# Memory key steps between the row tiles of the output projection, later transposes behind it, more weight chunks in work, and every low part on VectorE

## The chip, the cores and the metric

The kernel runs on one core of one Trainium2 chip. The metric is device time in microseconds of one execution, the median of several runs; less is better. Engines are named as in the profile: PE is TensorE's matmul (PEld its weight load), DVE is VectorE, ACT is ScalarE, POOL is GpSimd and SP is SyncE, which issues the loads.

## The reference

Two layers of a decoder trunk, batch 1, 512 tokens, width 1024, all in float32. Each of a layer's three parts ends in a LayerNorm of `alpha * x + f(x)`:

```python
for l in range(DEPTH):                       # 2
    h = hybrid_mixer(x, ...)                 # u = x @ w_in; branches A, B, C; merged @ w_out
    x = layer_norm(alpha * x + h, ...)
    x = layer_norm(alpha * x + memory_cross_attention(x, mem, xq, xkv, xo), ...)
    x = layer_norm(alpha * x + swiglu(x, w_up, w_down), ...)
```

Branch A is differential attention, C a dilated window attention, and B a recurrence whose two gates come of block-diagonal 64 x 64 products of a convolved input. The three are projected, gated and summed; `w_out` (1024 x 1024) follows. Cross-attention has 4 heads over 256 memory tokens: `k, v = split(mem @ xkv)`, and q comes from the new x. The feed-forward part is 2816 wide.

## The kernel before

**Precision.** PE works on pairs. Every operand is split into a high part in the fast float format (`xh`, `whi`) and a low part, the float32 value less the high part (`xl`, `wlo`). A product is three matmuls: high x high, high x low and low x high.

**Weights.** All weights lie in memory as 371 chunks of 128 x 1024, in the order of their use. For each chunk SP loads `raw` (`load_raw`, L264), ACT casts it to `whi` (`split_chunk`, L272), and `flush` (L282) makes `wlo` by a subtraction at L284: on DVE, but on POOL for the chunks in `on_pool` (L258), which are the memory key chunks 2 to 7 and the first four of `w_up`, ten per layer. `refill` (L289) casts the next chunks after a step, at most two, as long as fewer than `pairs` of the step are in work; `flush` follows after the step's matmuls are written. Loads run three chunks ahead of the casts.

**Steps.** `make_program` (L57) writes out the order of all steps by hand. Kind "a" is one output tile of 128 columns with the weights stationary (`tile_step`, 24 matmuls, 512 wide, or 256 for the memory); kind "b" is one row tile of 128 tokens and 512 columns (`group`, one step for each of the four row tiles, 24 matmuls); "k" does two slices of the contraction for all four rows. A step's result is used by its `post` function, which is written when the next step is. Every engine works through its own list in the order in which it is written, so an instruction waits for all that stands before it on its engine.

**The output projection.** The steps of a layer go: branches; two memory key steps; `w_out` for columns 0 to 511 (four rows) and for 512 to 1023 (four rows); the other six memory key steps; memory values (four rows); queries `xq`. `post_memk` casts a key tile on ACT (`mkh`) and subtracts on DVE (`mkl`). `post_ln` (L688) adds a row to x on DVE (L695) and takes its statistics; at the second half of a row it starts `ln_item` (L487): aggregate, a power on POOL (L492), and two passes over 1024 columns on DVE (L495, L497). `ln_item` then waits some turns (`waits`, L698: three for the first LayerNorm, one or two for the others) before it issues eight transposes of the row on PE (L510), and four casts (ACT) and four subtractions (DVE, L517) make the new `xh` and `xl`. The queries need all four rows. The second LayerNorm (behind `xo`) goes the same way; the first up steps after it take rows 0 and 1 first.

**Branch B.** For each of eight tiles of 128 channels `b_item` (L522) casts the convolved input into `xs`, copies halves across by DMA, and subtracts the two halves of `pad` (64 x 512 each): one on POOL (L534), one on DVE (L535). Four matmuls follow (`z`, L539 and L540). POOL also does `ti` (L565), `bl` (L575), `acc` (L646) and two rotary products per tile (L585, L586).

Of the kernel before, what the change touches and what calls it, by code (L numbers as in the profile page):

```python
# [17 lines left out]
P = 128  # L18
# [38 lines left out]
def make_program():  # L57
# [10 lines left out]
    def tile_step(name, l, c0, act, post, n0=0, n1=S, **kw):  # L68
        c = ch(name, l, 0, KT, c0, P)
        st = Step("a", [c], act=act, post=post, nk=KT, ncol=P, off=0, n0=n0, n1=n1, **kw)  # L70
        steps.append(st)
        return st

    def group(name, l, k0, nk, c0, act, post, pairs, tokens=NT, needs=None, pre=None):
        cs = [ch(name, l, k0 + 2 * k, 2, c0, 512) for k in range(nk // 2)]
        for t in range(tokens):
            st = Step("b", cs, act=act, post=post + (t,), t=t, pairs=pairs)
            if needs:
                st.need = tuple(n.format(t=t) for n in needs)
            if pre and t == 0:  # L80
                st.pre = pre
            steps.append(st)

    for l in range(L):
        def a_head(h, pairs):
# [54 lines left out]
        for n in range(KT):  # L140
            tile_step("w_br_b", l, P * n, "oB", ("merge", l, "B", n), need=("oB%d" % l,),
                      pre=("mem", l) if n == 5 else None)
        for kt in range(2):
            tile_step("xkv", l, P * kt, "mem", ("memk", l, kt), n0=0, n1=MEM, pairs=5)
        for h in range(2):
            group("w_out", l, 0, KT, 512 * h, "m", ("ln", l, 1, h), 5,
                  needs=("m%d" % l,))
        for kt in range(2, KT):
            tile_step("xkv", l, P * kt, "mem", ("memk", l, kt), n0=0, n1=MEM, pairs=5)
        for h in range(2):  # L150
            group("xkv", l, 0, KT, D + 512 * h, "mem", ("memv", l, h), 5, tokens=2)
        for kt in range(KT):
# [2 lines left out]
        for h in range(4):  # L155
            steps.append(Step("k", [ch("xo", l, 2 * h, 2, 0, 512)], act="ox", k0=2 * h,
                              post=("lns", l, 2, 0) if h == 3 else None, pairs=4,
                              need=("ox%d_%d" % (l, h),)))
        group("xo", l, 0, KT, 512, "ox", ("ln", l, 2, 1), 6)
        for gi, (j0, nj) in enumerate(GROUPS):  # L160
            if gi == 0:
                cs = [ch("w_up", l, 0, KT, HID * (i % 2) + P * (i // 2), P) for i in range(4)]
# [17 lines left out]
def kernel(  # L180
# [72 lines left out]
    for s, st in enumerate(steps):  # L253
        for c in st.chunks:
            last_use[c] = s
            if first_use[c] is None:
                first_use[c] = s
    on_pool = {c for c, (name, l, k0, nk, c0, n) in enumerate(chunks)  # L258
               if (name == "xkv" and 2 * P <= c0 < D) or (name == "w_up" and c0 % HID < 2 * P)}
    raws, hi, lo, late = {}, {}, {}, []  # L260
    ptr = {"raw": 0, "split": 0}
    RAW_AHEAD = 3
# [9 lines left out]
    def split_chunk(s):  # L272
        c = ptr["split"]
        while ptr["raw"] <= c:
            load_raw()
        h, lw, raw = a4("whi", [1024], F32R), a4("wlo", [1024], F32R), raws.pop(c)
        A.copy(h, raw)  # L277
        hi[c], lo[c] = h, lw
        late.append((lw, raw, h, G if c in on_pool else V))
        ptr["split"] += 1  # L280

    def flush():  # L282
        for lw, raw, h, eng in late:
            eng.tensor_tensor(lw, raw, f(h), ALU.subtract)  # L284
        late.clear()
        while ptr["raw"] < min(NCH, ptr["split"] + RAW_AHEAD):
            load_raw()
# [199 lines left out]
    def ln_item(l, which, t, waits):  # L487
        st, xt = lnst.pop(t), x_res[t]
        gb, bb = lnp["g"], lnp["b"]
        V.bn_aggr(st[:, 12:14], st[:, 0:12])  # L490
        V.tensor_scalar(st[:, 14:15], st[:, 13:14], EPS_LN, None, ALU.add)  # L491
        G.tensor_tensor(st[:, 15:16], st[:, 14:15], expo, ALU.pow)  # L492
        last = l == L - 1 and which == 3
        for c in (slice(0, 512), slice(512, 1024)) if last else (slice(0, 1024),):
            V.scalar_tensor_tensor(xt[:, c], xt[:, c], st[:, 12:13], gb[:, c],  # L495
                                   ALU.subtract, ALU.mult)
            V.scalar_tensor_tensor(xt[:, c], xt[:, c], st[:, 15:16], bb[:, c],  # L497
                                   ALU.mult, ALU.add)
            if last:
                nc.sync.dma_start(out[t * P:(t + 1) * P, c], xt[:, c])  # L500
        if last:
            return
        for _ in range(waits):
            yield
        if t == 0:
            new_act("x", KT)
        for q in range(2):
            tp = bank("tp")
            for k in range(4):
                T.transpose(tp[:, k * P:(k + 1) * P],  # L510
                            xt[:, (4 * q + k) * P:(4 * q + k + 1) * P], ident)
            for k in range(2):
                xh, xl = acts["x"][2 * q + k]
                src = tp[:, 2 * k * P:2 * (k + 1) * P].rearrange("p (a b) -> p a b", a=2)
                dh, dl = xh[:, :, t * P:(t + 1) * P], xl[:, :, t * P:(t + 1) * P]
                A.copy(dh, src)  # L516
                V.tensor_tensor(dl, src, f(dh), ALU.subtract)  # L517
        mark("x%d_%d_%d" % (l, which, t))
# [3 lines left out]
    def b_item(l, n):  # L522
# [8 lines left out]
        nc.sync.dma_start(f(xs[w, 0, :]), f(xs[u, 0, :]))  # L531
        nc.sync.dma_start(f(xs[u, 1, :]), f(xs[w, 1, :]))
        xl = padded()
        G.tensor_tensor(xl[u, 0, :], xc[u], f(xs[u, 0, :]), ALU.subtract)  # L534
        V.tensor_tensor(xl[w, 1, :], xc[w], f(xs[w, 1, :]), ALU.subtract)  # L535
        yield
        z = [bank("z0"), bank("z1")]
# [150 lines left out]
    def post_ln(ps, l, which, half, t):  # L688
# [6 lines left out]
        V.scalar_tensor_tensor(xs, ps, co, xs, ALU.mult, ALU.add)  # L695
        V.bn_stats(lnst[t][:, 6 * half:6 * half + 6], xs)
        if half == 1:
            waits = 3 if which == 1 else 2 if t == NT - 1 else 1  # L698
            g = ln_item(l, which, t, waits)
            if step_side(g):  # L700
                fresh.append(g)
# [358 lines left out]
```

## Time and profile before

| | |
|---|---|
| median of 3 runs | 2204.24 us (2202.59 to 2205.01) |
| the profiled execution | 2206.34 us, span 2204.6 us |
| PE busy | 2176.7 us |
| DVE busy | 1229.3 us |
| ACT busy | 927.2 us |
| POOL busy | 314.9 us |
| low parts (L284) on DVE | 351, mean 1273 ns |

Times in rows are microseconds from the first instruction of the profiled execution. Busy time of PE overlaps itself: matmuls are pipelined and their ends are modelled, so the distance of two starts tells more than one duration. Idle time is put down to the instruction that released the wait last. `PEclk` is the clock that TensorE was granted, as a share of full speed.

### The profile page before, as it was taken

Reading aid. Unit: us, or ns where it says so; the run is one execution under the profiler, and the core shown is the slowest. Engines: PE = TensorE matmul, PEld = TensorE weight load, DVE = VectorE, ACT = ScalarE, POOL = GpSimd, SP = SyncE. Lnnn points to the kernel's source line nnn. Section 1 sums busy time; section 2 is a strip of 40 time slices with the busy share of each in tenths; the row PEclk is TensorE's granted clock in tenths of the full one; section 3 lists DMA queues with packets and bytes.
Section 4 is the critical chain, followed back from the end, with each engine's and each line's share of the span. In section 5 each row is a group of like instructions: output and inputs, shape, how many; then the busy total and the mean of one; then the engine's idle time right before and its main releaser. Section 6 shows DMA issues by size and latency. Waiting matters only on the chain.

```text
span 2204.6 us, 26795 instructions
## 1 busy us (share of the span) xinstructions
PE 2176.7 (99%) x10516; PEld 1812.0 (82%) x10516; DVE 1229.3 (56%) x2014; ACT 927.2 (42%) x1647; POOL 314.9 (14%) x224
## 2 busy tenths in 40 slices
PE   9999999999999999999999999999999999999998
PEld 6888888788887888888888888887888878888887
DVE  6566666746746733243557676576466466332435
ACT  4445686643334222132135556766333333221330
POOL 3113213310300300000012132032103002000000
PEclk9999999999999999999999999999999999999999
DMA  7213333334332322242242223223334223223321
GB/s 257 79 58 100 96 91 96 117 96 146 107 113 96 108 84 86 69 148 88 72 144 77 66 85 101 85 86 129 105 125 143 86 86 125 78 76 132 97 96 39
DMA packets 65278, 224.37 MB, mean 102 GB/s; under 512 B 7936, under 2 KB 7936, under 8 KB 65152
## 3 DMA queue, kind: packets, MB, share of 16 engines
q1 hardware_dynamic: 65152, 222.66, 31.0%
q8 instruction: 83, 1.36, 0.2%
q14 instruction: 43, 0.35, 0.0%
HBM read 212.14 MB, written 2.10 MB: 97 GB/s over the span
## 4 chain that ended last, share of the span: by engine, by line
PE 70%; issue 22%; POOL 4%; DVE 3%; ACT 1%; DMA 0%; POOLq 0%; SPq 0%; ACTq 0%
PE ps L832 17%; PE ps L831 17%; PE ps L833 16%; PE ps L864 5%; PE ps L862 5%; PE ps L863 5%; POOL wlo L284 2%; PE o L429 1%; PE tp L423 1%; PE sc L356 1%; PE sc L355 1%; POOL ln L492 1%; PE o L385 1%; DVE x L497 1%; POOL bl L575 1%
## 5 line engine op out<-in xcount | busy, mean ns | idle before, releaser
L831 PE MATMUL ps<-xh,whi 128*128 128x512 f32 (+1 forms) x1792 | 695.8, 388 | 2.2 <-ACT xh L891 2.1
L832 PE MATMUL ps<-xl,whi 128*128 128x512 f32 (+1 forms) x1792 | 689.1, 385 | 0.6 <-DVE xl L769 0.5
L833 PE MATMUL ps<-xh,wlo 128*128 128x512 f32 (+1 forms) x1792 | 688.0, 384 | 1.3 <-POOL wlo L284 1.3
L284 DVE TENSOR_TENSOR wlo<-raw,whi 128x1024 fp32r<-128x1024 f32 x351 | 441.7, 1273 | 49.8 <-ACT whi L277 42.3
L277 ACT CAST whi<-raw 128x1024 fp32r<-128x1024 f32 x371 | 382.1, 1045 | 149.2 <-PE ps L863 96.9
L833 PEld LDWEIGHTS ps<-xh,wlo 128*128 128x128 f32 x1792 | 338.9, 189 | 68.6 <-POOL wlo L284 2.1
L831 PEld LDWEIGHTS ps<-xh,whi 128*128 128x128 f32 x1792 | 339.0, 189 | 68.1 <-ACT xh L891 4.4
L832 PEld LDWEIGHTS ps<-xl,whi 128*128 128x128 f32 x1792 | 339.1, 189 | 64.4 <-DVE xl L769 1.0
L492 POOL TENSOR_TENSOR ln<-ln,expo 128x1 f32<-128x1 f32 x24 | 33.8, 1410 | 1182.1 <-DVE ln L491 1182.1
L862 PE MATMUL ps<-whi,hh 128*128 128x512 f32 x352 | 137.3, 390 | 0.0
L863 PE MATMUL ps<-wlo,hh 128*128 128x512 f32 x352 | 137.1, 390 | 0.0
L864 PE MATMUL ps<-whi,hl 128*128 128x512 f32 x352 | 137.1, 390 | 0.0
L759 ACT CAST hh<-fg 128x512 fp32r<-128x512 f32 x44 | 27.3, 620 | 191.8 <-DVE fg L758 191.8
L516 ACT CAST xh<-tp 128x256 fp32r<-128x256 f32 x80 | 28.0, 376 | 178.4 <-PE tp L510 101.3
L748 DVE SCALAR_TENSOR_TENSOR fg<-fg,ps 128x512 f32<-128x512 f32 x44 | 30.3, 688 | 116.9 <-ACT fg L747 116.9
L758 DVE TENSOR_TENSOR fg<-fg,ps 128x512 f32<-128x512 f32 x44 | 30.3, 688 | 114.4 <-PE ps L833 114.4
L747 ACT ACTIVATE fg<-ps 128x512 f32<-128x512 f32 x44 | 26.3, 598 | 135.0 <-PE ps L833 135.0
L585 POOL TENSOR_TENSOR raw<-raw,tabs 128x512 f32<-128x512 f32 x32 | 42.7, 1335 | 254.1 <-ACT raw L582 254.1
L695 DVE SCALAR_TENSOR_TENSOR x<-ps,x 128x512 f32<-128x512 f32 x48 | 33.0, 687 | 80.5 <-PE ps L864 80.4
L863 PEld LDWEIGHTS ps<-wlo,hh 128*128 128x128 f32 x352 | 66.1, 188 | 13.7
L862 PEld LDWEIGHTS ps<-whi,hh 128*128 128x128 f32 x352 | 66.1, 188 | 13.6
L864 PEld LDWEIGHTS ps<-whi,hl 128*128 128x128 f32 x352 | 66.1, 188 | 13.6
(235 smaller groups left out, 3511.7 us busy)
## 6 DMA issues: line engine op xcount, KB each, us to landing
raw<-in_wts_dram SPq DMA_DIRECT2D x371, 512.0 KB, 3.6
xs<-xs SPq DMA_DIRECT2D x32, 128.0 KB, 2.2
lng<-in_lnp_in_dram SPq DMA_DIRECT2D x6, 512.0 KB, 5.0
lnb<-in_lnp_in_dram SPq DMA_DIRECT2D x6, 512.0 KB, 5.7
tabs<-in_tabs_in_dram SPq DMA_DIRECT2D x4, 512.0 KB, 8.9
x<-in_x_in_dram SPq DMA_DIRECT2D x4, 512.0 KB, 8.7
qkA<-qkA SPq DMA_DIRECT2D x16, 128.0 KB, 2.2
qkC<-qkC SPq DMA_DIRECT2D x16, 128.0 KB, 2.2
```

The lines of the kernel that those rows point to most:

```text
L277: A.copy(h, raw)
L284: eng.tensor_tensor(lw, raw, f(h), ALU.subtract)
L492: G.tensor_tensor(st[:, 15:16], st[:, 14:15], expo, ALU.pow)
L585: G.tensor_tensor(raw, raw, tab[:, 0, :], ALU.mult)
L695: V.scalar_tensor_tensor(xs, ps, co, xs, ALU.mult, ALU.add)
L748: V.scalar_tensor_tensor(g, g, 1.0, ps, ALU.add, ALU.mult)
L831: T.matmul(pv, wh, xh, start=(kt == 0), stop=False)
L832: T.matmul(pv, wh, xl, start=False, stop=False)
L833: T.matmul(pv, wl, xh, start=False, stop=(kt == st.nk - 1))
L862: T.matmul(ps, xh, wh, start=(i == 0), stop=False)
L863: T.matmul(ps, xh, wl, start=False, stop=False)
L864: T.matmul(ps, xl, wh, start=False, stop=(i == n - 1))
```

## The change

Four things change. (1) Of the six late memory key steps five now stand between the rows of the second half of `w_out`: one behind row 0, two behind row 1, one behind row 2, two behind row 3. (2) The first LayerNorm's transposes wait until the last row of `w_out` has been taken up (mark `rows`), and row t then for t turns more. (3) `pairs`, the number of chunks in work, goes from 5 to 6 in these steps and from 6 to 8 in the second half of `xo`. (4) `on_pool` is gone: all low parts of weights are made on DVE, as is the other half of `pad`: per layer ten subtractions of 128 x 1024 and eight of 64 x 512 move from POOL to DVE. The list of loads on SP keeps its order.

```diff
+    def group(..., pre=None, between=None):
...
             steps.append(st)
+            if between:
+                between[t]()
...
-        for kt in range(2):
-            tile_step("xkv", l, P * kt, "mem", ("memk", l, kt), n0=0, n1=MEM, pairs=5)
-        for h in range(2):
-            group("w_out", l, 0, KT, 512 * h, "m", ("ln", l, 1, h), 5,
-                  needs=("m%d" % l,))
-        for kt in range(2, KT):
-            tile_step("xkv", l, P * kt, "mem", ("memk", l, kt), n0=0, n1=MEM, pairs=5)
+        def memk(*kts):
+            for kt in kts:
+                tile_step("xkv", l, P * kt, "mem", ("memk", l, kt), n0=0, n1=MEM, pairs=6)
+
+        memk(0, 1)
+        group("w_out", l, 0, KT, 0, "m", ("ln", l, 1, 0), 6, needs=("m%d" % l,))
+        group("w_out", l, 0, KT, 512, "m", ("ln", l, 1, 1), 6, needs=("m%d" % l,),
+              between=(lambda: memk(2), lambda: memk(3, 4), lambda: memk(5), lambda: memk(6, 7)))
...
-        group("xo", l, 0, KT, 512, "ox", ("ln", l, 2, 1), 6)
+        group("xo", l, 0, KT, 512, "ox", ("ln", l, 2, 1), 8)
...
-    on_pool = {c for c, (name, l, k0, nk, c0, n) in enumerate(chunks)
-               if (name == "xkv" and 2 * P <= c0 < D) or (name == "w_up" and c0 % HID < 2 * P)}
...
-        late.append((lw, raw, h, G if c in on_pool else V))
+        late.append((lw, raw, h))
...
-        for lw, raw, h, eng in late:
-            eng.tensor_tensor(lw, raw, f(h), ALU.subtract)
+        for lw, raw, h in late:
+            V.tensor_tensor(lw, raw, f(h), ALU.subtract)
...
             return
+        if which == 1:
+            while not met("rows%d" % l):
+                yield
+            waits = t
         for _ in range(waits):
...
-        G.tensor_tensor(xl[u, 0, :], xc[u], f(xs[u, 0, :]), ALU.subtract)
+        V.tensor_tensor(xl[u, 0, :], xc[u], f(xs[u, 0, :]), ALU.subtract)
...
-            waits = 3 if which == 1 else 2 if t == NT - 1 else 1
+            waits = 2 if t == NT - 1 else 1
+            if which == 1 and t == NT - 1:
+                mark("rows%d" % l)
```

The order of the instructions is made by this list of steps, so three places of it are shown, all in layer 0. Tile names carry a running number; `x_66` to `x_69` are rows 0 to 3 of x. Line numbers from L74 on are larger by up to 7 in the changed kernel.

On PE, at the end of row 0 of the second half of `w_out` (`mh`, `ml` are here the merged activations, 512 wide; the memory is 256 wide). Before, row 1 follows:

```order
L862 MATMUL ps_891_4726<-whi_885_4711,mh_847_4468 128x512
L863 MATMUL ps_891_4726<-wlo_886_4712,mh_847_4468 128x512
L864 MATMUL ps_891_4726<-whi_885_4711,ml_848_4469 128x512
L862 MATMUL ps_894_4761<-whi_868_4581,mh_811_4240 128x512
L863 MATMUL ps_894_4761<-wlo_869_4582,mh_811_4240 128x512
L864 MATMUL ps_894_4761<-whi_868_4581,ml_812_4241 128x512
```

Now memory key step 2 follows, which needs the low part `wlo_893`:

```order
L869 MATMUL ps_891_4726<-whi_886_4714,mh_847_4468 128x512
L870 MATMUL ps_891_4726<-wlo_887_4715,mh_847_4468 128x512
L871 MATMUL ps_891_4726<-whi_886_4714,ml_848_4469 128x512
L838 MATMUL ps_898_4770<-mh_834_4390,whi_892_4751 128x256
L839 MATMUL ps_898_4770<-ml_835_4391,whi_892_4751 128x256
L840 MATMUL ps_898_4770<-mh_834_4390,wlo_893_4752 128x256
```

Rows and key steps now alternate; the number of matmuls is the same.

On DVE, behind the last pass over row 3 in the first LayerNorm (`xl` are the splits of a transposed row, `mkl` the key tiles, `wlo` the low parts). Before:

```order
L497 SCALAR_TENSOR_TENSOR x_69<-x_69,ln_4723,lnb_4620 128x1024
L517 TENSOR_TENSOR xl_4867<-tp_4874,xh_4866 128x2x128
L517 TENSOR_TENSOR xl_4869<-tp_4874,xh_4868 128x2x128
L517 TENSOR_TENSOR xl_4871<-tp_4883,xh_4870 128x2x128
L517 TENSOR_TENSOR xl_4873<-tp_4883,xh_4872 128x2x128
L723 TENSOR_TENSOR mkl_4542<-ps_4892,mkh_4541 128x256
L723 TENSOR_TENSOR mkl_4542<-ps_4931,mkh_4541 128x256
L517 TENSOR_TENSOR xl_4867<-tp_4970,xh_4866 128x2x128
L517 TENSOR_TENSOR xl_4869<-tp_4970,xh_4868 128x2x128
L517 TENSOR_TENSOR xl_4871<-tp_4979,xh_4870 128x2x128
L517 TENSOR_TENSOR xl_4873<-tp_4979,xh_4872 128x2x128
L284 TENSOR_TENSOR wlo_4966<-raw_4958,whi_4965 128x1024
```

Now:

```order
L498 SCALAR_TENSOR_TENSOR x_69<-x_69,ln_4723,lnb_4623 128x1024
L522 TENSOR_TENSOR xl_5005<-tp_5012,xh_5004 128x2x128
L522 TENSOR_TENSOR xl_5007<-tp_5012,xh_5006 128x2x128
L522 TENSOR_TENSOR xl_5009<-tp_5021,xh_5008 128x2x128
L522 TENSOR_TENSOR xl_5011<-tp_5021,xh_5010 128x2x128
L285 TENSOR_TENSOR wlo_4992<-raw_4891,whi_4991 128x1024
L285 TENSOR_TENSOR wlo_4995<-raw_4924,whi_4994 128x1024
L730 TENSOR_TENSOR mkl_4544<-ps_5030,mkh_4543 128x256
L285 TENSOR_TENSOR wlo_5062<-raw_4989,whi_5061 128x1024
L285 TENSOR_TENSOR wlo_5065<-raw_5057,whi_5064 128x1024
L730 TENSOR_TENSOR mkl_4544<-ps_5069,mkh_4543 128x256
```

The two pairs of `wlo` are the low parts of the first memory value rows; they now stand between row 3 and the splits of row 1, and the six key tiles' low parts, which POOL made before, stand further up on DVE.

On DVE in the second LayerNorm, behind the last pass over row 1 (L497, now L498). Before, the splits of row 0 are followed by row 2:

```order
L497 SCALAR_TENSOR_TENSOR x_67<-x_67,ln_6111,lnb_6107 128x1024
L517 TENSOR_TENSOR xl_6197<-tp_6204,xh_6196 128x2x128
L517 TENSOR_TENSOR xl_6199<-tp_6204,xh_6198 128x2x128
L517 TENSOR_TENSOR xl_6201<-tp_6213,xh_6200 128x2x128
L517 TENSOR_TENSOR xl_6203<-tp_6213,xh_6202 128x2x128
L695 SCALAR_TENSOR_TENSOR x_68<-ps_6222,x_68 128x512
```

Now a pair of low parts of `w_up` stands between:

```order
L498 SCALAR_TENSOR_TENSOR x_67<-x_67,ln_6111,lnb_6107 128x1024
L522 TENSOR_TENSOR xl_6203<-tp_6210,xh_6202 128x2x128
L522 TENSOR_TENSOR xl_6205<-tp_6210,xh_6204 128x2x128
L522 TENSOR_TENSOR xl_6207<-tp_6219,xh_6206 128x2x128
L522 TENSOR_TENSOR xl_6209<-tp_6219,xh_6208 128x2x128
L285 TENSOR_TENSOR wlo_6190<-raw_6102,whi_6189 128x1024
L285 TENSOR_TENSOR wlo_6193<-raw_6185,whi_6192 128x1024
L700 SCALAR_TENSOR_TENSOR x_68<-ps_6228,x_68 128x512
```

Another pair stands in the same way behind row 0's last pass, ahead of row 1. Before, these four were made on POOL. The order of the transposes among the rows and up steps on PE is the same as before in this place.

## Rows read from the trace of the kernel before

**Rows 1.** The page, part 1: busy us (share of the span) and instructions
```profile
PE 2176.7 (99%) x10516; PEld 1812.0 (82%) x10516; DVE 1229.3 (56%) x2014; ACT 927.2 (42%) x1647; POOL 314.9 (14%) x224
```

**Rows 2.** Waits of PE: engine, line <- waited for: us in total, times, longest
```profile
PE ps L833 <- POOL wlo L284: 5.0, 6, 1.9
...
PE z L540 <- POOL pad L534: 4.4, 2, 2.2
...
PE tp L510 <- DVE x L497: 3.1, 2, 1.5
```

**Rows 3.** Timeline of PE, last B gates of layer 0: start, us, what [idle before <-releaser]
```profile
437.56 0.39 PE L833 MATMUL ps<-xh,wlo 128*128 128x512 f32 x1
...
437.79 0.39 PE L539 MATMUL z<-xs,gw 128*128 128x512 f32 x1
...
440.40 0.50 PE L540 MATMUL z<-pad,gw 128*128 128x512 f32 x1 [2.22 <-POOL pad L534]
```

**Rows 4.** Timeline of PE in a memory key step of layer 0
```profile
577.48 0.28 PE L831 MATMUL ps<-mh,whi 128*128 128x256 f32 x1
...
577.60 0.28 PE L832 MATMUL ps<-ml,whi 128*128 128x256 f32 x1
...
579.75 0.39 PE L833 MATMUL ps<-mh,wlo 128*128 128x256 f32 x1 [1.88 <-POOL wlo L284]
```

**Rows 5.** Sums by window: us, then PE, PEld, DVE, ACT, POOL busy, PEclk, DMA share, GB/s
```profile
441.10:444.50 3.40, 3.40 (x10) 2.65 (x9) 1.02 (x2) 3.31 (x5) 0.00 (x0) 0.50 0.59 176
...
581.10:584.50 3.40, 3.40 (x18) 3.40 (x18) 1.19 (x4) 2.81 (x5) 2.69 (x2) 0.51 0.37 141
...
727.00:731.00 4.00, 4.00 (x22) 3.45 (x23) 3.45 (x6) 0.37 (x1) 3.63 (x2) 1.00 0.57 176
```

**Rows 6.** A `pad` half on DVE and PE's use of it (timelines); all of L535, ns min/median/max
```profile
350.47 0.69 DVE L535 TENSOR_TENSOR pad<-xc,xs 64x512 fp32r<-64x512 f32 x1
...
352.79 0.39 PE L540 MATMUL z<-pad,gw 128*128 128x512 f32 x1
...
L535 DVE TENSOR_TENSOR pad<-xc,xs x16: 687/1266/1672, 281.2 to 1526.6; 64x512 fp32r<-64x512 f32 x16
```

**Rows 7.** Timeline of DVE: low parts in a row, and row evacuations of the output projection
```profile
529.24 4.62 DVE L284 TENSOR_TENSOR wlo<-raw,whi 128x1024 fp32r<-128x1024 f32 x4
...
552.16 0.69 DVE L695 SCALAR_TENSOR_TENSOR x<-ps,x 128x512 f32<-128x512 f32 x1 [0.63 <-PE ps L864]
...
557.60 0.69 DVE L695 SCALAR_TENSOR_TENSOR x<-ps,x 128x512 f32<-128x512 f32 x1 [4.02 <-PE ps L864]
```

**Rows 8.** Timelines of DVE and (723.43) POOL in layer 0's second LayerNorm
```profile
720.01 0.69 DVE L695 SCALAR_TENSOR_TENSOR x<-ps,x 128x512 f32<-128x512 f32 x1 [2.60 <-PE ps L864]
...
723.50 3.40 DVE L497 SCALAR_TENSOR_TENSOR x<-x,ln,lnb 128x1024 f32<-128x1024 f32 x1 [0.44 <-POOL ln L492]
...
723.43 5.71 POOL L284 TENSOR_TENSOR wlo<-raw,whi 128x1024 fp32r<-128x1024 f32 x2
...
730.66 1.29 DVE L497 SCALAR_TENSOR_TENSOR x<-x,ln,lnb 128x1024 f32<-128x1024 f32 x1 [0.44 <-POOL ln L492]
...
731.87 0.42 DVE L517 TENSOR_TENSOR xl<-tp,xh 128x256 fp32r<-128x256 f32 x1
...
734.26 0.68 DVE L695 SCALAR_TENSOR_TENSOR x<-ps,x 128x512 f32<-128x512 f32 x1
...
744.80 3.41 DVE L497 SCALAR_TENSOR_TENSOR x<-x,ln,lnb 128x1024 f32<-128x1024 f32 x1 [0.44 <-POOL ln L492]
```

**Rows 9.** Timeline of PE in the same stage
```profile
725.02 0.39 PE L864 MATMUL ps<-whi,oxl 128*128 128x512 f32 x1
...
726.95 1.09 PE L510 MATMUL tp<-ident,x 128*128 128x128 f32 x8 [1.54 <-DVE x L497]
...
739.73 1.04 PE L510 MATMUL tp<-ident,x 128*128 128x128 f32 x8
...
740.52 0.36 PE L831 MATMUL ps<-xh,whi 128*128 128x256 f32 x1
```

More of the change, by code (lines that the diff above doesn't have):

```diff
@@ L72, in tile_step, with group @@
         return st
-    def group(name, l, k0, nk, c0, act, post, pairs, tokens=NT, needs=None, pre=None):
+    def group(name, l, k0, nk, c0, act, post, pairs, tokens=NT, needs=None, pre=None, between=None):
         cs = [ch(name, l, k0 + 2 * k, 2, c0, 512) for k in range(nk // 2)]
```

## Prediction

> **What bounds the kernel now.** The page comes first: TensorE (PE) is busy for 2176.7 us, 99% of the span [rows 1], so only PE's waits can be won, and what counts of any other engine is whether it is late for PE. The next view is the list of PE's waits [rows 2]: GpSimd (POOL) is named in the two longest. Six waits for a low part `wlo` made by POOL cost 5.0 us, two for a `pad` made by POOL 4.4 us; transposes waiting for a LayerNorm row on VectorE (DVE) come third, 3.1 us. A matmul's end is modelled later than the start of the next one, so a wait's cost is its idle time and about 0.16 us more: in the timeline of PE the matmuls stand 0.12 us apart while one lasts 0.28, and the 1.88 us before 579.75 are 2.15 - 0.12 = 2.03 us from start to start [rows 4]; the 2.22 us before 440.40 are 2.61 - 0.23 = 2.38 [rows 3].
>
> Last, the same stretches in the sums by window, for the clock [rows 5]. Behind the wait at 440.40 the granted clock is 0.50 (1.2 of 2.4 GHz) for 3.4 us, behind the one at 579.75 it is 0.51 for as long. Such a stretch does 1.7 us of work in 3.4: **1.7 us lost behind each**. Behind the wait of 1.54 us at 726.95 the clock stays at 1.00 [rows 5, 9]. The `pad` wait and the 1.88 us wait each occur in both layers, so four times 1.7 us are lost in this way.
>
> **What the change removes.**
> 1. *The two `pad` waits.* `b_item` now makes both halves of `pad` on DVE. Cost before: 2 x (2.38 + 1.7) = 8.2 us. A half takes DVE 0.69 us [rows 6]; the tightest of the 16 places I found has the DVE half start at 350.47 and PE ask at 352.79 [rows 6], so two halves (1.4 us, 351.9) still leave 0.9 us. Added DVE time is hidden under PE's running steps there; without that cover it would cost 0.69 us a place. **-8.2 us.**
> 2. *The wait in the memory key steps*, 2 x (2.03 + 1.7) = **-7.5 us**, before what takes its place.
> 3. *The other four `wlo` waits*, two per layer in the first up steps: 5.0 - 2 x 1.88 = 1.24 us idle, with 0.16 us for each 1.9 us: **-1.9 us**.
> 4. *The wait at 726.95*, 1.54 + 0.16 = 1.70 us in each layer [rows 9], **-3.4 us**. It comes of POOL too: the DVE instruction L497 that it waits for took 3.40 us, starting 0.07 us behind a POOL low part, where its like takes 1.29 [rows 8]. Without POOL it ends at 723.50 + 1.29 = 724.79, and PE is there at 725.25 (its last matmul starts at 725.02 [rows 9], and they stand 0.23 apart [rows 3]).
>
> Removed: 21.0 us.
>
> **What it adds.** DVE gets 20 low parts at 1.13 us (four in 4.62 us [rows 7], each start 1.13 behind the last) and 16 halves at 0.69, 33.6 us in all. It costs only where PE arrives first, and this I followed by hand in the two stages where the low parts now stand in front of a LayerNorm row or behind it.
>
> *Memory stage, layer 0.* A `w_out` row is 5.44 us (552.16 to 557.60, both waiting for PE [rows 7]), a memory key step 24 x 0.12 = 2.88. In the new order rows 1 to 3 of the second half and key steps 2 to 5 follow the row whose evacuation is at 557.60, so row 3 is evacuated at 557.60 + 3 x 5.44 + 4 x 2.88 = 585.44. A LayerNorm row holds DVE 3.49 us to the start of L497 (720.01 to 723.50) and 1.21 more (730.66 to 731.87); the four splits of a transposed row take 2.39 (731.87 to 734.26) [rows 8]. So the first low part of the memory values starts at 585.44 + 4.70 + 2.39 = 592.53 and, at 1.22 us, is there at 593.75. PE, which ended the row 0.22 before its evacuation, does 0.8 of transposes (739.73 to 740.52 [rows 9]), two key steps, 0.8 again, and asks 0.23 into the next row: 592.81. **A new wait of 0.9 us**, with sight of the semaphore 1.0; the next three low parts come 1.13 to 2.6 us behind it, and PE needs one every 1.36, so there is no second one. The 1.54 us wait left the clock at full, so only 2 x 1.0 = **+2.0 us**. Left out of it: the moved transposes do the same PE work as before, and the last have two memory value rows (10.9 us) for 2.39 us of splits.
>
> *Second LayerNorm, layer 0.* Two low parts stand behind row 0's L497 and two behind its splits. DVE is free at 723.50 + 1.21 = 724.71, then 2 x 1.13, row 1 from 726.97, its L497 starts 3.49 later at 730.46 and ends at 731.75. PE arrives at 725.25 + 0.8 + 5.44 and some 0.1 = 731.6: a wait of 0.15. Row 2 then has 2.39 of splits and 2.26 of low parts in front of it: it starts at 730.46 + 1.21 + 2.39 + 2.26 = 736.32 and is there 3.49 + 1.29 later, at 741.1. PE arrives at 731.8 + 0.8 + 5.5 = 738.1: **a new wait of 3.0 us**. It is longer than the waits behind which the clock fell, so I add 1.7: 0.15 + 3.0 + 1.7 = 4.85 per layer, **+9.7 us**. In the trace of before PE came to this place at 739.73 and did not wait.
>
> *More chunks in work* (limits 6 and 8) lets ScalarE cast `whi` earlier. The order of the load queue is unchanged; the casts are on ScalarE, which is 42% busy [rows 1], and the low parts lose their cover only as counted. Bounds: nothing, to one such wait of 1 us per layer; I take nothing. *Key steps between the rows* add no PE work.
>
> **Sum:** -21.0 + 2.0 + 9.7 = **-9.3 us**. The profiled execution took 2206.34 us (span and 1.7 around it), 2.1 above the median of 2204.24. So 2197.0 for its like and **2194.9 us as a median**.
>
> **A rule against one part of it.** In the second LayerNorm DVE is the engine that PE waits for, and the change hands it four more low parts there. The row shows that POOL held DVE up by 2.1 us there (3.40 against 1.29 [rows 8]), against 2 x 1.13 us for doing the pair itself. The Trainium skill, Perfetto Trace Analysis, section Optimizing Scalar/DVE Operations, says to consider offloading to GpSimd when DVE is saturated, but adds that the two share a read port, so that moving work between them might not help. By that clause the stage would come out even, and the sum would be about -13.7 us. The rows make the stage 2.2 us dearer per layer (4.85 for the 1.70 and 0.95 removed there), since two pairs now stand ahead of row 2 and PE arrives sooner; I go by the rows.
>
> **Rivals.**
> - *The clock holds behind the new 3.0 us wait.* For it: the 1.54 us wait left it at 1.00, and the trace has no wait of 3 us in the body. Against: two waits of 1.88 and two of some 2.2 us all brought it down. It gives -12.7 us, 2191.5; one layer of two, 2193.2.
> - *The second LayerNorm comes out even*: the hold-ups that go (2.1 us of DVE at row 0, and one more of this kind at row 3) make up for the four low parts (4.5 us), and row 2 is no later than PE. -9.3 - 2 x 2.2 = -13.7 us, 2190.5. Against: row 3's hold-up comes behind row 2, too late to help it. It is the outcome of the clause named above.
> - *DVE becomes the bound.* The place is the two LayerNorm stages, where it runs nearly without a pause. The price is at most the 33.6 us of added work against the 21.0 removed: +12.6 us, 2216.8. It ends slower than before once over 62% of the added DVE time lands on PE's path; I count 2.0 + 6.3 = 8.3 us of it, a quarter. For it: the margins in the memory stage are tenths of a us. Against: it needs several waits more per layer than the hand count finds.
> - *New waits eat most of it*: one more wait with a clock drop in each layer, at the low parts of the memory values, 2 x (1.0 + 1.7) = +5.4: -3.9 us, 2200.3.
> - *The change does not do what it says*: beside its remaining work (`acc`, `ti`, `bl`) POOL still holds up the halves of `pad`. At the worst of L535 (1.67 us before) both halves take 3.3 and one wait of 1.0 us comes back per layer: -7.3 us, 2196.9.
>
> **How the numbers follow.** The forecast (with the last rival, which lies inside it) 0.64; the clock holding once or twice 0.14; the second LayerNorm even 0.04; new waits that eat most 0.12; DVE the bound 0.06. The range takes in the first three and stops short of the fourth: 2190 to 2200. A measurement of this kernel can tell about 0.2%, 4.4 us, from no change. Faster by more: 0.64 + 0.14 + 0.04 and a third of the fourth, 0.86; within: 0.09; slower: 0.05.
>
> **What would show it.** In the changed kernel's profile: POOL is gone from PE's waits; both `pad` waits and the half clock behind them have vanished; PE waits some 1.0 us for a DVE low part at the first memory value row, and some 3 us for L498 at row 2's transposes in the second LayerNorm, with half clock behind it in both layers; L498 takes 1.28 us there throughout. I am wrong if that wait is under 2 us, if the clock falls in the memory stage, or if PE waits for `pad` again.

## The result, and the profile after

The changed kernel took 2193.05 us (median of 4 runs, 2190.88 to 2194.9), the kernel before 2204.55 in the same comparison: ratio 0.9949, interval 0.9932 to 0.9966. The forecast was 2194.9, range 2190 to 2200. Measured again beside a later run, the changed kernel took 2195.11 us (5 runs, 2194.09 to 2195.57), ratio 0.9965 (0.9951 to 0.9978). The nine runs together have their median at 2194.8.

The page of the changed kernel, part 1, against [rows 1]:

```profile
PE 2171.1 (99%) x10516; PEld 1807.0 (82%) x10516; DVE 1236.3 (56%) x2050; ACT 926.6 (42%) x1647; POOL 238.0 (11%) x188
```

The 36 instructions are on DVE now (2050 for 2014) and gone from POOL (188 for 224). POOL's busy time fell by 76.9 us; DVE's rose by 7.0 only.

What PE waits for, against [rows 2] (us in total, times, longest):

```profile
PE tp L515 <- DVE x L498: 5.5, 2, 2.8
...
PE ps L870 <- DVE wlo L285: 1.3, 2, 0.6
```

No line names POOL any more, neither for a low part nor for a `pad`. Two places are left that the change made: the transposes of row 2 in the second LayerNorm (row 1 adds 0.20 us), and the first memory value row.

The memory stage, layer 0: first the timeline of DVE from row 3's last pass to the memory value low parts, then that of PE.

```profile
583.25 1.28 DVE L498 SCALAR_TENSOR_TENSOR x<-x,ln,lnb 128x1024 f32<-128x1024 f32 x1 [0.44 <-POOL ln L493]
...
586.50 0.43 DVE L522 TENSOR_TENSOR xl<-tp,xh 128x256 fp32r<-128x256 f32 x1 [0.44 <-ACT xh L521]
586.84 2.35 DVE L285 TENSOR_TENSOR wlo<-raw,whi 128x1024 fp32r<-128x1024 f32 x2
```

```profile
586.98 0.48 PE L869 MATMUL ps<-whi,mh 128*128 128x512 f32 x1
588.11 0.50 PE L870 MATMUL ps<-wlo,mh 128*128 128x512 f32 x1 [0.65 <-DVE wlo L285]
```

Start to start the two matmuls stand 1.13 us apart where full pace is 0.23: a wait of 0.90 us, for the pair that starts at 586.84 behind the splits. In layer 1 it is 0.90 as well.

The second LayerNorm, layer 0, against [rows 8, 9]: DVE's last passes over rows 0, 1 and 2 with the pairs of low parts between them, and PE.

```profile
715.03 1.29 DVE L498 SCALAR_TENSOR_TENSOR x<-x,ln,lnb 128x1024 f32<-128x1024 f32 x1 [0.44 <-POOL ln L493]
716.24 2.36 DVE L285 TENSOR_TENSOR wlo<-raw,whi 128x1024 fp32r<-128x1024 f32 x2
...
721.99 1.28 DVE L498 SCALAR_TENSOR_TENSOR x<-x,ln,lnb 128x1024 f32<-128x1024 f32 x1 [0.44 <-POOL ln L493]
...
725.58 2.35 DVE L285 TENSOR_TENSOR wlo<-raw,whi 128x1024 fp32r<-128x1024 f32 x2
...
731.33 1.28 DVE L498 SCALAR_TENSOR_TENSOR x<-x,ln,lnb 128x1024 f32<-128x1024 f32 x1 [0.44 <-POOL ln L493]
```

```profile
729.51 0.39 PE L871 MATMUL ps<-whi,oxl 128*128 128x512 f32 x1
732.66 1.95 PE L515 MATMUL tp<-ident,x 128*128 128x128 f32 x8 [2.77 <-DVE x L498]
```

All passes take 1.28 or 1.29 us; the 3.40 us of [rows 8] are gone. PE is there at 729.51 + 0.23 = 729.74 and starts at 732.66, 2.92 us later. Behind it stands the clock; sums by window (us, PE, PEld, DVE, ACT, POOL busy, PEclk, DMA share, GB/s), here behind row 2's wait in both layers and behind the memory value wait:

```profile
732.70:736.10 3.40, 3.40 (x16) 3.40 (x17) 2.49 (x6) 2.58 (x5) 0.00 (x0) 0.50 0.64 261
1821.50:1824.90 3.40, 3.40 (x19) 3.40 (x18) 2.86 (x8) 2.53 (x4) 0.30 (x1) 0.51 0.64 261
588.20:591.60 3.40, 3.40 (x15) 2.82 (x16) 3.40 (x4) 2.87 (x6) 0.00 (x0) 1.00 0.05 16
```

Half clock for 3.4 us behind the wait of 2.9 us, full clock behind that of 0.9.

**A measure free of the start.** The first 20 us (loads, first matmuls) differ between executions by some 2 us, whatever the kernel. PE's first `ot` transpose stands behind them; here before, then changed, in layers 0 and 1:

```profile
94.16 0.27 PE L396 MATMUL ot<-ident,on 128*128 128x128 f32 x1
...
1188.06 0.27 PE L396 MATMUL ot<-ident,on 128*128 128x128 f32 x1
```

```profile
92.54 0.27 PE L397 MATMUL ot<-ident,on 128*128 128x128 f32 x1
...
1181.46 0.27 PE L397 MATMUL ot<-ident,on 128*128 128x128 f32 x1
```

From the first `ot` to the end of the span: before 2204.6 - 94.16 = 2110.4, changed 2193.0 - 92.54 = 2100.5. The change is worth **-9.9 us**, 5.0 from the one `ot` to the other (1093.90 against 1088.92) and 4.9 behind it. This length is called the body below; a second profile of the changed kernel (e10_same) has 2100.4. A body still holds the half clocks that its execution happened to have, so these have to be looked up before two bodies are compared. In the same way the stages of a layer can be compared, by the starts of PE's matmuls (us in layer 0, layer 1):

| | first `ot` to last `z<-pad` | to the first use of a query (`xqh`) | to the first `w_down` matmul |
|---|---|---|---|
| before | 346.81, 345.83 | 198.03, 197.74 | 236.27, 236.26 |
| changed | 344.31, 343.13 | 193.77, 193.76 | 238.05, 237.99 |
| e5_dve_only | 344.33, 343.15 | 198.71, 199.38 | 239.56, 238.07 |
| e6_order_only | 346.99, 345.59 | 195.32, 193.85 | 236.65, 236.68 |
| e7_pad_pool | 346.89, 345.60 | 195.33, 193.80 | 239.31, 238.15 |
| e2_fill | 344.33, 343.11 | 193.79, 193.77 | 236.56, 236.59 |
| e3_up_pool | 344.33, 343.16 | 193.75, 193.78 | 236.61, 236.68 |
| e1_hold | 344.37, 343.16 | 193.77, 193.78 | 234.69, 234.69 |
| e9_hold_all | 344.41, 343.16 | 192.85, 192.85 | 233.33, 233.30 |

The first two columns (the `pad` wait, its half clock, the key steps, less the new memory value wait) gave 13.4 us over the two layers, the third, with the second LayerNorm, took 3.5 back. From the first `w_down` matmul to the next layer or the end, all these profiles agree within 0.05 us, so the table holds the whole difference.

### The profile page after: what moved, and what is told of

Read it like the earlier page. It is cut to its first block, busy times and chain, and to the rows that moved or that the text cites. A ratio compares the mean times of both kernels' runs of the same rounds, so it can differ in the third digit from the quotient of the medians.

```text
span 2193.0 us, 26730 instructions
## 1 busy us (share of the span) xinstructions
PE 2171.1 (99%) x10516; PEld 1807.0 (82%) x10516; DVE 1236.3 (56%) x2050; ACT 926.6 (42%) x1647; POOL 238.0 (11%) x188
## 4 chain that ended last, share of the span: by engine, by line
PE 94%; DVE 3%; ACT 1%; POOL 1%; issue 0%; DMA 0%; SPq 0%; POOLq 0%; ACTq 0%; DVEq 0%
PE ps L839 21%; PE ps L838 21%; PE ps L840 21%; PE ps L870 7%; PE ps L871 7%; PE ps L869 7%; PE o L430 1%; PE tp L424 1%; PE sc L357 1%; PE sc L356 1%; PE ps L853 1%; PE ps L851 1%; PE o L386 1%; PE ps L852 1%; DVE wlo L285 1%; POOL ln L493 1%
## 5 line engine op out<-in xcount | busy, mean ns | idle before, releaser
L285 DVE TENSOR_TENSOR wlo<-raw,whi 128x1024 fp32r<-128x1024 f32 x371 | 461.3, 1259 | 47.4 <-ACT whi L278 40.0
L871 PEld LDWEIGHTS ps<-whi,hl 128*128 128x128 f32 x352 | 66.1, 188 | 13.7
L870 PE MATMUL ps<-wlo,mh 128*128 128x512 f32 x192 | 75.0, 391 | 1.3 <-DVE wlo L285 1.3
```

Of the source, the lines that this page charges most:

```text
L285: V.tensor_tensor(lw, raw, f(h), ALU.subtract)
L870: T.matmul(ps, xh, wl, start=False, stop=False)
L871: T.matmul(ps, xl, wh, start=False, stop=(i == n - 1))
```

## The experiments

| run | what is different | median us (range, runs) | ratio to before | body |
|---|---|---|---|---|
| e10_same | changed kernel again | 2195.11 (2194.09 to 2195.57, 5) | 0.9965 [0.9951, 0.9978] | 2100.4 |
| e5_dve_only | before, with only low parts and pad on DVE | 2207.99 (2207.29 to 2212.31, 6) | 1.0029 [1.0017, 1.0041] | 2112.7 |
| e6_order_only | changed, low parts and pad on POOL | 2198.99 (2196.73 to 2199.66, 11) | 0.9986 [0.9977, 0.9994] | 2104.5 |
| e7_pad_pool | changed, pad half on POOL | 2201.14 (2198.18 to 2204.16, 11) | 0.9991 [0.9982, 1.0] | 2108.5 |
| e3_up_pool | changed, w_up's low parts on POOL | 2191.74 (2191.17 to 2192.63, 5) | 0.9952 [0.9939, 0.9965] | 2097.8 |
| e8_xo6 | changed, limit 6 in xo | 2197.7 (2196.07 to 2199.35, 11) | 0.9978 [0.9969, 0.9987] | 2103.6 |
| e2_fill | changed, PE kept busy in the wait | 2191.97 (2191.19 to 2192.66, 5) | 0.9952 [0.9939, 0.9965] | 2097.6 |
| e1_hold | changed, one pair moved | 2187.62 (2187.58 to 2188.88, 5) | 0.9935 [0.9922, 0.9947] | 2093.9 |
| e4_hold_memv | e1_hold and limit 7 | 2185.76 (2185.16 to 2186.27, 6) | 0.9923 [0.9911, 0.9936] | 2091.8 |
| e9_hold_all | e4_hold_memv and three low parts later | 2183.12 (2182.78 to 2183.44, 4) | 0.9911 [0.9897, 0.9924] | 2089.4 |

Most expectations start from 2193.05 us, the median of four runs of which two have a mean granted clock of 0.999. e10_same has 0.996 in all five runs and 2195.11, so a time some 2 us above an expectation is no miss by itself. Where a time alone would not tell theory from rival, the waits and the clock in the trace decide.

**Either half of the change alone.** e5_dve_only takes the kernel before and moves the work, no step:

```diff
-        late.append((lw, raw, h, G if c in on_pool else V))
+        late.append((lw, raw, h, V))
-        G.tensor_tensor(xl[u, 0, :], xc[u], f(xs[u, 0, :]), ALU.subtract)
+        V.tensor_tensor(xl[u, 0, :], xc[u], f(xs[u, 0, :]), ALU.subtract)
```

> The kernel before with only the move of the low parts and of the pad halves from GpSimd to VectorE; steps, transposes and chunks in work stay as before. Theory (VectorE alone is not enough, the order has to give it time): the pad waits go, -8.2 us. In the memory stage the low part of key step 3 now stands on VectorE behind row 3's chain and row 0's splits: row 3 is evacuated at 574.1, + 4.70 + 2.39 + 1.13 = 582.3, TensorE asks at 577.7, a wait of 4.6 us where there were 2.04, +5.2 over two layers. In the second LayerNorm row 2 comes 0.6 us late and the third up step waits 3.7 us for its low part with half clock behind it, 6.2 us per layer where there were 2.65, +7.1. Sum +4.1: slower, about 2208. Rival (the move to VectorE is what brought the gain, the order is beside the point): all waits for GpSimd go, 2193 or less.

Measured 2207.99, slower than before. Its longest line of PE's waits:

```profile
PE ps L833 <- DVE wlo L284: 15.8, 4, 4.4
```

Start to start they are 4.56 and 3.68 us in layer 0 (expected 4.6 and 3.7), and the `pad` waits are gone. By the body it is 2.3 us slower, not 4.1; most of the missing 1.8 is a half clock that did not come behind the fourth wait (at 1841.5, last section). The rival falls: with only the engine changed, the low parts are later on DVE than they were on POOL.

e6_order_only keeps the new order and gives POOL its work back (the two lines above the other way round, and `on_pool` as before).

> The changed kernel with all low parts and pad halves back on GpSimd as in the kernel before, so only the order, the later transposes and the chunks in work are changed. Theory (the key steps between the rows give even GpSimd time, 2.7 us for a low part against a row of 5.44 us): no wait in the key steps, the pad waits stay (8.2 us), the second LayerNorm is that of the run with w_up's low parts on GpSimd (2.7 us less than the changed kernel): 2193.05 + 8.2 - 2.7 = 2198.5. Rival (GpSimd is too slow there in any order): the key steps' wait and half clock come back as well, + 7.5, 2206.

Measured 2198.99. Its waits:

```profile
PE tp L517 <- DVE x L500: 5.3, 6, 1.5
PE z L547 <- POOL pad L541: 4.4, 2, 2.2
```

No key step waits for POOL. So the 7.5 us of step 2 (the wait in the memory key steps) do not need DVE: with the new order, the later transposes and limit 6 together, POOL's low parts are in time. The body is 4.0 us above the changed kernel's, not 5.5, because in this execution only layer 0's `pad` wait was followed by half clock (second column: 195.32 and 193.85).

Which of the three did it was not separated. The trace of before shows that POOL was not too slow there: it stood idle for 3.3 us, and the low part of key step 3 came behind the power of row 3 (L492) on its queue, though its `whi` was there (ACT casts no weights from 551.23 to 582.61 us).

```profile
561.03 2.39 POOL L284 TENSOR_TENSOR wlo<-raw,whi 128x1024 fp32r<-128x1024 f32 x1
...
575.86 1.52 POOL L492 TENSOR_TENSOR ln<-ln,expo 128x1 f32<-128x1 f32 x1 [3.31 <-DVE ln L491]
577.35 5.68 POOL L284 TENSOR_TENSOR wlo<-raw,whi 128x1024 fp32r<-128x1024 f32 x2
```

The first is key step 2's low part, the last line begins with key step 3's, asked for at 577.7. By the rule of `refill`, limit 6 in the old order would cast key chunk 3 together with key chunk 2 and so write its low part ahead of the powers of rows 1 to 3. That limit 6 alone would have removed the wait is therefore a rival that no run here tests; nor was the new order run with limit 5, or the later transposes by themselves. (Not five but four of the six late key steps, 2 to 5, stand between the rows; 6 and 7 follow row 3.)

**The pad halves.** e7_pad_pool puts back only `G.tensor_tensor(xl[u, 0, :], ...)`.

> The changed kernel with only the one half of pad back on GpSimd. Theory (this half was late because of what stands ahead of it on GpSimd, acc and bl, which are still there): both waits of 2.38 us at the last B gates with 1.7 us of half clock each come back, + 8.2 us, 2201.2. Rival (it was late because GpSimd had the low parts too): no wait at the B gates, 2193.

Measured 2201.14, body + 8.0. The waits are those of before (2.37 us start to start, where before has 2.38):

```profile
PE z L545 <- POOL pad L539: 4.4, 2, 2.2
```

It is what stands ahead on POOL (`acc`, `bl`) that made this half late, not the low parts. That the body comes so near the 8.2 us is partly luck. The two waits are 5.1 us of it (first column of the table), but only layer 0's was followed by half clock, 1.6 us (second column). The other 1.4 us lie in the third column: in this execution the half clock around row 2's wait in layer 0 lasted twice as long as in the changed kernel's profiles:

```profile
736.80:740.20 3.40, 2.73 (x13) 2.73 (x14) 2.52 (x6) 1.87 (x5) 0.00 (x0) 0.50 0.86 349
740.20:743.60 3.40, 3.40 (x18) 3.40 (x18) 2.85 (x6) 1.31 (x3) 1.52 (x1) 0.50 0.00 0
```

In the changed kernel DVE makes both halves at the same place in 1.77 and 1.67 us (432.14 and 433.95) while POOL works on `acc` and `bl` from 431.70 to 436.75, and PE asks at 436.40; that is 0.8 us to spare.

**The second LayerNorm.** e3_up_pool makes only the first four `w_up` low parts of each layer on POOL.

> The changed kernel with only the low parts of the first four chunks of w_up in each layer back on GpSimd; pad, the memory keys and the order stay as changed. Theory (VectorE's second LayerNorm is lengthened by the four low parts, and shortened by GpSimd's absence): the 2.93 us wait and its half clock go, the wait at row 0's transposes comes back with 1.70 us, with a 3.4 us pass on VectorE, and at most 0.95 us for GpSimd's low parts: 4.83 - 2.65 = 2.2 us less per layer, 2188.7 (2186.8 if the low parts, cast earlier now, are not waited for). Rival (it comes out even, what GpSimd does is paid by VectorE through what they share): within 1.5 us of 2193.

Measured 2191.74, body -2.7. PE waits three times per layer for a row of DVE:

```profile
717.83 1.09 PE L517 MATMUL tp<-ident,x 128*128 128x128 f32 x8 [1.54 <-DVE x L500]
...
725.01 1.09 PE L517 MATMUL tp<-ident,x 128*128 128x128 f32 x8 [0.59 <-DVE x L500]
...
732.08 1.09 PE L517 MATMUL tp<-ident,x 128*128 128x128 f32 x8 [0.52 <-DVE x L500]
```

Row 0's wait is back with 1.70 us and a pass of 3.40 us on DVE, as forecast, no low part is waited for and the clock stays at full. What I had not counted are 0.75 us at row 1 and 0.68 at row 2: cast earlier, POOL's second pair (721.48, 5.71 us) now holds up row 1's pass too (3.41 us). 3.1 us per layer: neither even with DVE nor the 2.65 that I took. The time alone lies within the rival's 1.5 us of 2193; the stage table decides against it: the stage is 1.4 us shorter per layer than in the changed kernel.

e8_xo6 sets the limit in the second half of `xo` back from 8 to 6.

> The changed kernel with six chunks in work instead of eight in the second half of xo, as before. The third and fourth low part of w_up then stand on VectorE behind row 3's chain and row 2's splits. Theory (this limit is what keeps VectorE's low parts early enough): row 2's wait falls to 0.6 us with the clock at full, but the third up step waits for its low part: asked for at 737.2, ready at 730.26 + 2.39 + 4.70 + 2.39 + 1.13 = 740.9, 3.7 us and 1.7 us of half clock. 6.0 us per layer where the changed kernel has 4.83: 2193.05 + 2.4 = 2195.5. Rival (the limit is beside the point, as the prediction took it): the 4.05 us of the moved pair are won, 2185 to 2187.

Measured 2197.7, body + 3.1 (2.4 expected). The wait at the third up step is 3.68 us in layer 0, as worked out:

```profile
PE ps L840 <- DVE wlo L285: 7.0, 2, 3.5
```

with PEclk 0.59 in the 4 us behind it, and row 2 waits 0.66. The rival falls. The prediction took the limits at nothing; this one is worth 3 us, since it sets where the low parts stand on DVE.

e1_hold lets `flush` pass over two chunks once, so that their subtractions stand behind row 2's chain and the splits of row 1. No other engine's order changes.

```diff
+    hold = {c for c, (name, l, k0, nk, c0, n) in enumerate(chunks)
+            if name == "w_up" and c0 in (P, HID + P)}
...
-        late.append((lw, raw, h))
+        late.append([lw, raw, h, 1 if c in hold else 0])
...
-        for lw, raw, h in late:
-            V.tensor_tensor(lw, raw, f(h), ALU.subtract)
-        late.clear()
+        for e in list(late):
+            if e[3]:
+                e[3] -= 1
+                continue
+            V.tensor_tensor(e[0], e[1], f(e[2]), ALU.subtract)
+            late.remove(e)
```

> The changed kernel with one thing moved: in each layer the low parts of the third and fourth chunk of w_up are written one turn later, so that on VectorE they stand behind the chain of row 2 of the second LayerNorm and no longer in front of it. Nothing else moves on any engine. Theory (the wait of 2.93 us at row 2's transposes is these two subtractions, 2.35 us, and the half clock behind it is its consequence): the wait shrinks to 2.93 - 2.35 = 0.58 us, the clock stays at full, 2.35 + 1.7 = 4.05 us less per layer, 2193.05 - 8.1 = 2185.0. Rival A (the pair only moves the wait on to the third up step, which needs the third chunk): a new wait at the third up step, the time within 1.5 us of 2193. Rival B (the clock falls after any wait here): only 2 x 2.35 = 4.7 us less, 2188.4.

Measured 2187.62, body -6.6. Row 2's transposes now start at 731.20 behind 0.50 us of idle time, and the clock stays:

```profile
731.20 0.98 PE L520 MATMUL tp<-ident,x 128*128 128x128 f32 x7 [0.50 <-DVE x L503]
```

```profile
731.20:735.20 4.00, 4.00 (x34) 4.00 (x35) 3.12 (x6) 3.15 (x6) 0.00 (x0) 1.00 0.86 324
```

So these two subtractions were the wait, and the half clock was its consequence. No new wait comes at the third up step, so rival A falls; the time alone lies nearest rival B's 2188.4, but B needs half clock behind the wait, and the clock stays at 1.00. The stage is 3.3 us shorter per layer, not 4.05: the wait went by 2.27 us (2.93 to 0.66), the half clock was worth 1.45 (e2_fill, below), and 0.36 come back later, where the first up step on rows 2 and 3 waits 0.70 us for its split instead of 0.34, since PE arrives sooner and DVE does not. 2.27 + 1.45 - 0.36 = 3.36.

e2_fill separates the wait from the clock: the wait stays, but PE works in it.

```diff
         for q in range(2):
             tp = bank("tp")
+            if which == 2 and t == 2 and q == 0:
+                for k in range(26):
+                    T.transpose(tp[:, (k % 4) * P:(k % 4 + 1) * P],
+                                x_res[1][:, (k % 8) * P:(k % 8 + 1) * P], ident)
```

> The changed kernel with 26 transposes of row 1 (0.109 us each, 2.8 us) written ahead of row 2's transposes in the second LayerNorm; they go into the same bank and are overwritten, so TensorE works through the wait on VectorE instead of standing still. Theory (the wait costs 2.93 us and on top of it 1.7 us of half clock): the wait is gone from the list, row 2's transposes start at the same time as before, the half clock behind them is gone, 2 x 1.7 = 3.4 us less, 2189.7. Rival (the half clock is not set by TensorE's idle time before it but comes of the transposes and short matmuls that follow): the half clock stays, 2193.0.

Measured 2191.97, body -2.9. Behind the place, in both layers:

```profile
732.50:735.90 3.40, 3.40 (x30) 3.22 (x29) 2.49 (x7) 2.21 (x5) 0.00 (x0) 1.00 0.77 311
1818.80:1822.20 3.40, 3.40 (x31) 3.23 (x29) 2.49 (x7) 2.28 (x5) 0.00 (x0) 1.00 0.72 294
```

The same steps at the same time run at 1.00 where they ran at 0.50: 30 matmuls in 3.4 us for 16. The rival falls, by the clock; the time alone lies between the two. The added transposes won 1.45 us per layer, not 1.7: behind row 2's transposes the matmuls are 256 wide, 0.21 us apart at half clock for 0.12 at full, which is less than double. The 512 wide ones behind the `pad` wait are 0.43 us apart for 0.23, less than double too; there one half clock cost 1.6 us (e7_pad_pool, second column).

**Better than both.** e4_hold_memv adds `pairs=7` in the memory key steps, so that the first memory value low part stands ahead of row 3.

> The move of the third and fourth low part of w_up one turn later as in the run beside it, and seven chunks in work instead of six in the memory key steps, which puts the low part of the first memory value chunk ahead of row 3 of the first LayerNorm on VectorE. Theory: the 0.58 us wait in the second LayerNorm as in the run beside it, and the 0.90 us wait for the first memory value chunk goes, as row 3 is not needed before three turns later: 8.1 + 2 x 0.9 = 9.9 us less, 2183.2. Rival (VectorE is full in the memory stage, and what is written earlier only moves the wait): a wait of about 1 us for the second value chunk or at row 3's transposes, 2185.0.

Measured 2185.76. This is 2.6 us above the theory, as e1_hold was, and near the rival's figure, but the rival's new wait did not come: against e1_hold the body is 2.1 us shorter, and the 0.90 us waits are gone.

e9_hold_all holds back three more low parts, `{HID: 2, P: 1, HID + P: 1, 2 * P: 5, HID + 2 * P: 5}` passes of `flush` by column offset.

> The run with held low parts and seven chunks in work, and beyond it in each second LayerNorm: the second low part of w_up also stands behind row 2's chain on VectorE, and the fifth and sixth stand behind row 3's splits. Theory (each of the small waits left there, 0.20 us at row 1, 0.66 at row 2 and 0.71 - 0.34 = 0.37 at the first up step on rows 2 and 3, is a low part in front of the row): they go, 1.2 us per layer, 2185.76 - 2.4 = 2183.4. Rival (VectorE is full there and what is moved behind a row is late for the up steps): a new wait for a low part at the second up step or at the fifth chunk, not below 2185.

Measured 2183.12, body 2.5 us below e4_hold_memv. From 715 to 745 us PE is busy for 29.9 of 30 us:

```profile
715.00:745.00 30.00, 29.90 (x202) 27.15 (x201) 23.44 (x39) 8.22 (x19) 4.56 (x3) 1.00 0.32 106
1797.00:1827.00 30.00, 29.90 (x201) 27.15 (x200) 23.51 (x39) 8.21 (x19) 4.56 (x3) 1.00 0.34 106
```

Of these kernels it is the fastest: by the body 21 us below before and 11 below the change.

e10_same is the changed kernel unaltered.

> The changed kernel once more, unaltered, on one chip with the run beside it. Both theories: the same waits on TensorE as in its first profile (0.90, 0.20 and 2.93 us per layer), 2193 within 2 us, where only the first 20 us may differ from run to run.

Its waits are 0.90, 0.20 and 2.93 us per layer again. Its median, 2195.11, is 0.1 us outside the stated 2 us.

## Why the prediction was right

- *The `pad` waits, -8.2.* Right in cause. The two waits gave 5.2 us (first column, before to changed) where 4.8 was put; each half clock was mis-sized at 1.7, e7_pad_pool shows 1.6. The cover was thinner than I read it: 0.69 us for a half is the least of [rows 6], whose median is 1.27. The halves took 3.4 us at the last gates, not the 1.4 I counted, and end 0.8 us ahead of PE. So the condition of the last rival, that POOL still holds the halves up, came true; its wait did not.
- *The key steps, -7.5.* Right: the wait is gone. The prediction did not say which part of the change removes it. e5_dve_only shows that DVE alone does not, e6_order_only that it goes without DVE; whether the order, limit 6 or both did it stays open.
- *The up steps' low parts, -1.9, and the wait at row 0, -3.4.* Both are gone; the pass that took 3.40 us takes 1.29, and e3_up_pool brings the 3.40 and the 1.70 us back.
- *The memory value wait, + 2.0.* 2 x 0.90 = 1.8, with the clock at full, as forecast.
- *The second LayerNorm, + 9.7.* Row 1 waits 0.20 us (0.15 said), row 2 2.93 (3.0), and the clock falls in both layers. The half clock is the term that was mis-sized: 1.45 us by e2_fill where 1.7 was put. Together 2 x (3.13 + 1.45) = 9.2. The clause weighed there (the Trainium skill, Perfetto Trace Analysis, section Optimizing Scalar/DVE Operations: moving work between DVE and GpSimd might not help) would, as the prediction applied it, have the stage come out even. On DVE's time alone it is near that: two passes shorter by 2.1 us each against four low parts of 1.13. For PE it is not, because the second long pass stood at row 3, behind the row that was late, and e1_hold shows that the place decides: the same work a few instructions later costs PE 3.3 us less per layer.
- *The chunks in work, 0.* The sum holds, but not because the limits do nothing: the cost that I gave to the low parts' new places is already the cost with limit 8, and e8_xo6 shows that 6 would have been dearer by 3.1 us. The limit 6 in the key steps may carry part of the -7.5, as said.
- *The sum.* -9.3 was forecast for the profiled execution's like; the body gives -9.9: -13.4 for the -13.7 of the first two columns, + 3.5 for the + 4.4 of the third. The profiled execution's 11.5 us (2206.34 to 2194.8) hold another 1.6 from the start, which the change does not touch.

Of the rivals, "the clock holds" was worked out at 2191.5. The mean granted clock of the first four runs is 0.996 twice (2194.8 and 2194.9 us) and 0.999 twice (2191.3 and 2190.9). That fits two executions in which it held in both layers; their timelines were not recorded, so this is argued, not shown. The forecast of 2194.9 is met by the two with 0.996; the median of 2193.05 lies between the two kinds. The other rivals fell.

## What to carry to other kernels

Moving work from an engine that is late to one that has time by its busy share helped here only where it stood behind what the bottleneck asks for first: the move alone was 2 us slower by the body and 5 by the medians, the reorder with its limits 6 and 4 us faster; by the body both together were 10 us faster, and with five low parts of each layer a few instructions later and limit 7 in the key steps 21 us. Follow each moved instruction to the first row behind it on its queue and to the time when the bottleneck asks for that row. Behind a wait on TensorE of 2.0 to 4.6 us half clock followed in 17 of 20 cases here, so such a wait is to be priced with it. Where the wait stayed, filling it with transposes that nobody reads was worth 1.45 us each time.

## What was not expected

**The clock does not always fall.** In the profiles of before, changed (both), e5, e6, e7 and e8 PE has 20 waits of 2.0 to 4.6 us, start to start, in its layers: four, four, four, two, four and two of them. With 17 of them the granted clock is 0.50 before 1.5 us have passed behind the wait, in four of these already within it; behind three it stays at 1.00. Two of the 17 half clocks last 6.8 us, the others 3.4. Behind the six waits of 1.70 us (before, e3 and e6) it stayed every time. Sums by window in e5_dve_only, behind its waits of 3.68 us in layer 0 and in layer 1:

```profile
746.80:750.80 4.00, 4.00 (x22) 4.00 (x23) 3.19 (x3) 0.09 (x1) 0.00 (x0) 0.58 0.40 135
...
1841.60:1845.60 4.00, 4.00 (x34) 4.00 (x35) 3.23 (x3) 0.13 (x1) 0.00 (x0) 1.00 0.40 131
```

The same wait in the same place of the program, and 22 matmuls in 4 us against 34. In e7_pad_pool the `pad` wait of 2.37 us brings half clock in layer 0 and none in layer 1. So the length of the wait does not settle it alone, and what does stays open. The spread of the times fits this: e7_pad_pool's 11 runs lie between 2198.2 us (mean clock 0.997) and 2204.2 (0.994).

**DVE got most of its new work for nothing.** By the estimate of the prediction 33.6 us of subtractions came to DVE, and its busy time rose by 7.0. The two halves of the change show how this splits (pages of e5_dve_only and e6_order_only, part 1):

```profile
PE 2173.7 (99%) x10516; PEld 1809.6 (82%) x10516; DVE 1237.4 (56%) x2050; ACT 927.8 (42%) x1647; POOL 238.1 (11%) x188
PE 2170.7 (99%) x10516; PEld 1805.1 (82%) x10516; DVE 1235.2 (56%) x2014; ACT 928.2 (42%) x1647; POOL 319.6 (15%) x224
```

In the old order the work adds 8.1 us to DVE's 1229.3, a quarter of its length. The new order with the work still on POOL adds 5.9 with no instruction more, and moving the work then adds 1.1. The rest had been hold-ups beside POOL, as far as the busy times tell; the 3.40 us passes of [rows 8] are some of them, and they are back in e3_up_pool with POOL's low parts. The clause of the Trainium skill named above (Perfetto Trace Analysis, section Optimizing Scalar/DVE Operations), that moving work between the two might not help, agrees with this for DVE's busy time: what POOL did saved DVE little.
